# Two-layer encoder trunk: the first two projection units run interleaved, k-tiles of x travel with their weight block, and products with the weights' low parts come last

## The chip, the cores and the metric

One core of a Trainium2 chip runs the whole kernel in one launch. The metric is device time in microseconds (us): the median over several runs. Engines are named as in the profile: PE (TensorE, matmul), PEld (its weight load), DVE (VectorE), ACT (ScalarE), POOL (GpSimd) and SP (SyncE, which here only issues DMAs).

## The reference, cut to what matters

A sequence of 256 frames with 2048 features passes layer A, then layer B. Both attend with 32 heads of 128.

```python
# layer A
h = rms_norm(x, a_norm)
q, k, v, g = split(h @ a_w_in, 4)                 # 2048 -> 4 x 4096
o = chunked_relbias_attention(q, k, v, a_rel_bias)
x = x + (o * silu(g)) @ a_w_out                   # 4096 -> 2048
# layer B
k, v = split(rms_norm(x, kv_norm) @ kv_w, 2)
logf = log_sigmoid(rms_norm(x, kv_norm) @ f_w + f_b)
q, g = split(rms_norm(x, b_norm) @ b_w_in, 2)
o = forgetting_attention(q, k, v, cumsum(logf))
x = x + (o * silu(g)) @ b_w_out
return rms_norm(x, final_norm)
```

Everything is float32. The per-row factor of the RMS norm (`rstd`) is applied after the product `h @ w`, so the projections can begin on `x` times the gain before the norm's sum is known.

## The kernel before, in words

**Products.** A float32 number is split into a high part (rounded to the matmul format `float32r`) and a low part (the rest). A product of two float32 tiles is made of three matmuls: high x high, high x low, low x high. `mm3` (L162-166) issues them for one k-tile (128 rows of the contraction) and one half `t` of the 256 frames. The stationary operand is a 128x128 tile of `x` (`xTh`, `xTl`); the moving one is a k-tile of weights of 512 columns.

**Units and blocks.** A unit is one 512-column slab of a projection: 16 k-tiles in layer A's and B's input projections. A unit has two PSUM accumulators, `acc[0]` and `acc[1]`, one for each half of the frames; the pool holds four. Weights come in blocks of two k-tiles (512 KB, `KB = 2`), so an input unit has 8 blocks of 12 matmuls. Layer A runs 32 units in the order `aqk0, avg0, aqk1, avg1, ...`: `aqk` gives q and k of two heads, `avg` gives v and gate of the same two. `Unit.step(b)` (L259) takes the next block from the feed and issues its 12 matmuls: for each k-tile, first half `t = 0` (three matmuls), then half `t = 1`.

**The feed.** `Feed` walks a list of (unit, block), `todo`, in the order in which the blocks are used. `load` (L178) allocates one of three raw buffers (`RAW = 3`) and issues the DMA on SP. `prepare` (L190) splits a block: ACT copies raw to `hi` (L204), DVE subtracts to get `lo` (L205); there are four slots each of `hi` and `lo` (`SPLIT = 4`), and preparation runs up to four blocks ahead. So the DMA of block n+3 waits for DVE's `lo` of block n, and the split of block n+4 waits for PE to finish block n.

**The start.** `x`, transposed, comes by `load_xT` (L427), and `split_xT` splits it (high part on ACT L142, or on DVE L140 for the first two k-tiles; low part on DVE L143). In the kernel before, k-tiles 0 to 3 are split between the first weight blocks, 4 to 7 after, and 8 to 15 come in two loads of four k-tiles each; the generator `first()` splits them and issues the loads of `x` in row layout (`xs`, 1 MB for each half, L449), from which `norm_a` (L434) makes the sums of squares on DVE and then `rstd` (L102 to L114, with a square root on ACT).

**The attention chain of a pair of heads.** It runs beside the units, in steps of a generator (`side_a`, `attention`):

1. ACT evacuates the `aqk` accumulators times `rstd` into `qk` (L317).
2. `turn` (L308, L312) transposes: DVE turns 32x32 pieces into `Y`, and POOL issues 16 DMAs that carry them into `Z`. Both have one buffer.
3. ACT and DVE split the turned q and k (`wideh`, `widel`, `q1h`, `q1l`: L326, L327), and PE makes the scores `s1p`, `s0p` (L331 to L333, L353).
4. DVE adds the bias and takes the maximum; ACT makes the exponentials (L363); ACT scales the gate (L374); a second `turn` (`sgY`, `sgZ`) transposes both.
5. ACT and DVE split the turned probabilities (`wideh`, `widel` again), PE multiplies them with v (`op`, L331 to L333, L386), and DVE multiplies with the gate (`oT`, L390), which frees `Z` for the next pair of heads.

`QK_STEPS` and `PV_STEPS` say after which block of the unit that PE is working on each of these steps is handed out. The place of each instruction in its engine's queue is then decided by a scheduler when the program is built, not by the text of the code alone. Each engine works through its queue in order.

Of the kernel before, what the change touches and what calls it, by code (L numbers as in the profile page):

```python
# [16 lines left out]
P = 128  # L17
S = 256
NT = S // P
# [11 lines left out]
KD = D // P  # L31
# [4 lines left out]
UN = 512  # L36
KB = 2
# [3 lines left out]
SPLIT = 4  # L41
DEPTH = 3
LATE = 8
KEPT = 5
BIG = 8
TERMS = 8
# [3 lines left out]
QK_STEPS = {0: 1, 6: 1, 7: 2}  # L50
PV_STEPS = {0: 1, 6: 1, 7: 2}
# [4 lines left out]
def r32(ap):  # L56
    return ap.bitcast(F32)
# [3 lines left out]
def trunk(ctx, tc, x, x_t, gains, a_w_in, a_rel, a_w_out, kv_w, f_w, f_b, b_w_in, b_w_out, final_norm, out):  # L61
    nc = tc.nc
    pe, act, dve, pool, sp = nc.tensor, nc.scalar, nc.vector, nc.gpsimd, nc.sync
# [16 lines left out]
    xf = x.rearrange("b (t p) d -> p (b t) d", p=P)  # L80
# [19 lines left out]
    def rstd_of(ssq, name):  # L100
        v = small.tile([P, NT], F32, name=f"v_{name}", tag="rs_v")
        dve.tensor_scalar(v, ssq, 1.0 / D, EPS, op0=OP.mult, op1=OP.add)  # L102
        sd = small.tile([P, NT], F32, name=f"sd_{name}", tag="rs_sd")
        act.activation(sd, v, AF.Sqrt)
# [9 lines left out]
        dve.tensor_scalar(hr, r, 0.5, None, op0=OP.mult)  # L114
        return r, hr
# [17 lines left out]
    def finish(side):  # L133
        advance(side, 99)
# [22 lines left out]
                split_x(dst, banks[c // 2][:, c % 2 * S:(c % 2 + 1) * S], k0 + c, g0)  # L157
            yield

    done = []  # L160

    def mm3(acc, lhs, k, t, hi, lo, nk):  # L162
        ts = slice(t * P, (t + 1) * P)
        pe.matmul(acc[t], lhs.h(k)[:, ts], hi, start=k == 0, stop=False)  # L164
        pe.matmul(acc[t], lhs.h(k)[:, ts], lo, start=False, stop=False)  # L165
        done.append(pe.matmul(acc[t], lhs.l(k)[:, ts], hi, start=False, stop=k == nk - 1))  # L166

    class Feed:

# [2 lines left out]
        def __init__(self, todo):  # L172
            self.todo = iter(todo)
            self.ready, self.loaded = [], []
            self.splits = []

        def load(self, spec, b, first):
            raw = stream.tile([P, KB, UN], F32, name=f"{spec['name']}_raw{b}", tag="raw", bufs=RAW)  # L178
            for j in range(KB) if first else [slice(None)]:
                if first:  # L180
                    first(j)
                sp.dma_start(out=raw[:, j], in_=spec["w"][b][:, j])
            return raw

        def begin(self, first=None):
            spec, b = next(self.todo, (None, 0))
            if spec:
                self.loaded.append((spec, b, self.load(spec, b, first)))

        def prepare(self, ahead=True, parts=(slice(None),)):  # L190
            if not self.loaded:
                self.begin()
            if not self.loaded:
                return
            spec, b, raw = self.loaded.pop(0)
            nm, h = spec["name"], b - (spec["nk"] // KB - spec["late"])
            if 0 <= h < spec["kept"]:
                both = big_tile([P, 2, KB, UN], F32R, f"{nm}_keep{b}")
                hi, lo = both[:, 0], both[:, 1]
            else:  # L200
                hi = stream.tile([P, KB, UN], F32R, name=f"{nm}_hi{b}", tag="hi", bufs=SPLIT)
                lo = stream.tile([P, KB, UN], F32R, name=f"{nm}_lo{b}", tag="lo", bufs=SPLIT)
            for j in parts:
                act.activation(hi[:, j], raw[:, j], AF.Copy)  # L204
                self.splits.append(dve.tensor_sub(lo[:, j], raw[:, j], r32(hi[:, j])))  # L205
# [25 lines left out]
    qkvg, todo = [], []  # L231
    for g in range(NG):
        qkvg.append(spec(f"aqk{g}", a_w_in[2 * g], KD))
        qkvg.append(spec(f"avg{g}", a_w_in[2 * g + 1], KD))
    ao = [spec(f"ao{u}", a_w_out[u], KI) for u in range(4)]
    for sp_ in qkvg + ao:
# [11 lines left out]
    feed = Feed(todo)  # L248
    order = iter(qkvg)

    class Unit:
# [8 lines left out]
        def step(self, b):  # L260
            hi, lo = feed.get()
            hold = b >= self.nk // KB - self.late
            if hold:
                self.held.append((b, hi, lo))
            for j in range(KB):
                for t in range(1 if hold else NT):
                    mm3(self.acc, self.lhs, b * KB + j, t, hi[:, j], lo[:, j], self.nk)
            self.left -= 1
            if not self.left:
                for b, hi, lo in self.held:  # L270
                    for j in range(KB):
                        mm3(self.acc, self.lhs, b * KB + j, 1, hi[:, j], lo[:, j], self.nk)

    def unit(lhs):
        u = Unit(lhs, next(order))
        for b in range(u.nk // KB):
            u.step(b)
            yield u.acc

# [153 lines left out]
    def norm_a():  # L433
        junk = att.tile([P, UN], F32, name="junk", tag="tb")  # L434
        for q in range(4):
            cs = slice(q * UN, (q + 1) * UN)
            for t in range(NT):
                dve.scalar_tensor_tensor(junk, xs[t][:, cs], 1.0, xs[t][:, cs],
                                         op0=OP.mult, op1=OP.mult, accum_out=ssq[:, t, q:q + 1])
        tot = const.tile([P, NT], F32, name="tot")  # L440
        dve.tensor_reduce(tot, ssq, axis=AX.X, op=OP.add)
        return rstd_of(tot, "a")

    def first():

        for k in range(4, KD, 2):
            split_xT(k, k + 2)
            if k < 8:
                sp.dma_start(out=xs[k // 2 - 2], in_=xf[:, k // 2 - 2])  # L449
            if k == KD - 2:  # L450
                rs.extend(norm_a())
            yield

    def halves():
        yield 0
        split_xT(1, 2, True)
        yield 1

    load_xT(0, 1)
    feed.begin(lambda j: load_xT(1, 2) if j else None)  # L460
    load_xT(2, 4)
    feed.begin()
    split_xT(0, 1, True)
    feed.prepare(False, halves())
    load_xT(4, 6)
    feed.begin()
    split_xT(2, 4)
    feed.prepare(False)
    load_xT(6, 8)
# [6 lines left out]
    rs = []  # L476
    ahead = first()

    oA = Stat("oA", KI)

# [32 lines left out]
    prev = None  # L513
    for g in range(NG):
        accs = {}
        accs["qk"] = drive(unit(xT),
                           prev if g else ahead, PV_STEPS if g else {i: 1 for i in range(7)})
        if g == 0:
            finish(ahead)
            rsA, halfA = rs  # L520
        finish(prev)
# [145 lines left out]
    prev = None  # L667
    fg = forget()
    for g in range(NG):
        accs = {}  # L670
# [4 lines left out]
        prev = side_b(g, accs)  # L675
# [96 lines left out]
```

## Time and profile before

| | us |
|---|---|
| median of 3 runs (lowest, highest) | 1859.43 (1858.83, 1859.74) |
| the profiled execution's own time | 1860.0 |
| its span, first to last instruction | 1858.3 |
| PE busy | 1840.2 |
| DVE busy | 1123.8 |
| ACT busy | 1008.2 |
| POOL busy | 542.6 |

The mean granted TensorE clock of the profiled execution is 0.996 of full speed, and the core's DMA engines move 214 GB/s on average, 281 GB/s in the first fortieth of the span. How to read a timeline row: start in us from the span's start, duration, engine, source line, operation, output <- inputs, size, how many instructions were merged into the row, and in brackets how long the engine had been idle and what ended that idle time. A matmul's duration overlaps the next one's, so the distance between starts is what counts.

### The profile page before, as it was taken

To read this page: it belongs to the slowest core of one execution; us is meant where nothing else is said; L and a number is where in the kernel's file an instruction comes from. 1 tells how busy PE (TensorE), PEld (TensorE's weight loads), DVE (VectorE), ACT (ScalarE), POOL (GpSimd) and SP (SyncE) were. 2 spreads that over 40 slices of the span, in tenths; PEclk is the share of its full clock that TensorE was granted. 3 is DMA by queue.
4 is the path that set the end of the run, shared out by engine and by line. 5 is a ranking of instruction groups with operands and counts; after the bars stand their busy time and mean duration, and the time that the engine had idled before them with its cause. 6 is when DMAs were issued, how large, how long until landed. Compare 5 with 4: busy or idle time off the path is not lost.

```text
span 1858.3 us, 25119 instructions
## 1 busy us (share of the span) xinstructions
PE 1840.2 (99%) x8395; PEld 1525.3 (82%) x8395; DVE 1123.8 (60%) x1450; ACT 1008.2 (54%) x1688; POOL 542.6 (29%) x1129
## 2 busy tenths in 40 slices
PE   8999999999999999999999999999999999999998
PEld 6888888888888888887888888888888888888886
DVE  6666656666666666555665666666665665655554
ACT  5555555555555555545555555555555655554443
POOL 0433333333333333111103333333333333333000
PEclk9999999999999999999999999999999999999999
DMA  8666666666676666666767666666666666676664
GB/s 281 216 216 210 212 214 219 214 208 217 215 212 210 217 215 212 208 218 222 230 185 220 209 216 215 216 217 213 214 214 218 214 213 213 212 235 214 207 203 161
DMA packets 141970, 398.43 MB, mean 214 GB/s; under 512 B 31088, under 2 KB 35472, under 8 KB 141456
## 3 DMA queue, kind: packets, MB, share of 16 engines
q1 hardware_dynamic: 106816, 356.35, 60.3%
q0 software_dynamic: 34304, 39.39, 6.6%
q8 instruction: 67, 1.10, 0.2%
q10 hardware_dynamic: 720, 1.07, 0.2%
q14 instruction: 63, 0.52, 0.1%
HBM read 353.15 MB, written 4.23 MB: 192 GB/s over the span
## 4 chain that ended last, share of the span: by engine, by line
PE 88%; DMA 5%; DVE 2%; POOL 2%; ACT 2%; issue 1%; SPq 0%; ACTq 0%; POOLq 0%; DVEq 0%
PE avg_acc L164 6%; PE bqg_acc L164 6%; PE bqg_acc L166 6%; PE bqg_acc L165 6%; PE avg_acc L165 6%; PE avg_acc L166 6%; PE bkv_acc L164 5%; PE bkv_acc L165 5%; PE bkv_acc L166 5%; PE aqk_acc L166 5%; PE aqk_acc L164 5%; PE aqk_acc L165 5%; PE bo_acc L166 3%; PE bo_acc L165 3%; PE bo_acc L164 3%; DMA sgZ<-sgY 2%
## 5 line engine op out<-in xcount | busy, mean ns | idle before, releaser
L312 POOL DMA_DIRECT2D sgZ<-sgY x512 | 250.5, 497 | 467.9 <-DVE sgY L308 410.1
L312 POOL DMA_DIRECT2D qkZ<-qkY x512 | 251.0, 497 | 379.4 <-DVE vl L405 97.3
L205 DVE TENSOR_TENSOR avg_lo<-avg_raw,avg_hi 128x1024 fp32r<-128x1024 f32 x128 | 156.5, 1223 | 130.3 <-ACT avg_hi L204 130.2
L205 DVE TENSOR_TENSOR bqg_lo<-bqg_raw,bqg_hi 128x1024 fp32r<-128x1024 f32 x128 | 156.6, 1223 | 129.4 <-ACT bqg_hi L204 129.4
L204 ACT ACTIVATE bqg_hi<-bqg_raw 128x1024 fp32r<-128x1024 f32 x128 | 135.4, 1058 | 143.2 <-PE bqg_acc L166 85.1
L204 ACT ACTIVATE avg_hi<-avg_raw 128x1024 fp32r<-128x1024 f32 x128 | 135.3, 1057 | 141.3 <-PE avg_acc L166 84.0
L205 DVE TENSOR_TENSOR aqk_lo<-aqk_raw,aqk_hi 128x1024 fp32r<-128x1024 f32 (+1 forms) x129 | 155.3, 1211 | 88.3 <-ACT aqk_hi L204 88.2
L164 PE MATMUL aqk_acc<-aqk_hi,xTh 128*128 128x512 f32 x512 | 202.2, 396 | 3.3 <-ACT xTh L142 3.0
L205 DVE TENSOR_TENSOR bkv_lo<-bkv_raw,bkv_hi 128x1024 fp32r<-128x1024 f32 x128 | 155.3, 1219 | 77.0 <-ACT bkv_hi L204 76.7
L166 PE MATMUL aqk_acc<-aqk_hi,xTl 128*128 128x512 f32 x512 | 200.6, 392 | 1.1 <-DVE xTl L143 1.1
L165 PE MATMUL aqk_acc<-aqk_lo,xTh 128*128 128x512 f32 x512 | 200.6, 392 | 1.1 <-DVE aqk_lo L205 1.1
L164 PE MATMUL bkv_acc<-bkv_hi,xkvh 128*128 128x512 f32 x512 | 201.1, 393 | 0.0
L164 PE MATMUL avg_acc<-avg_hi,xTh 128*128 128x512 f32 x512 | 200.7, 392 | 0.0
L164 PE MATMUL bqg_acc<-bqg_hi,xbh 128*128 128x512 f32 x512 | 200.7, 392 | 0.0
L166 PE MATMUL bqg_acc<-bqg_hi,xbl 128*128 128x512 f32 x512 | 199.5, 390 | 0.0
L166 PE MATMUL bkv_acc<-bkv_hi,xkvl 128*128 128x512 f32 x512 | 199.5, 390 | 0.0
L166 PE MATMUL avg_acc<-avg_hi,xTl 128*128 128x512 f32 x512 | 199.4, 389 | 0.0
L165 PE MATMUL bqg_acc<-bqg_lo,xbh 128*128 128x512 f32 x512 | 199.3, 389 | 0.0
L165 PE MATMUL avg_acc<-avg_lo,xTh 128*128 128x512 f32 x512 | 199.3, 389 | 0.0
L165 PE MATMUL bkv_acc<-bkv_lo,xkvh 128*128 128x512 f32 x512 | 199.2, 389 | 0.0
L204 ACT ACTIVATE aqk_hi<-aqk_raw 128x1024 fp32r<-128x1024 f32 (+1 forms) x129 | 134.8, 1050 | 86.2 <-PE aqk_acc L166 46.0
L204 ACT ACTIVATE bkv_hi<-bkv_raw 128x1024 fp32r<-128x1024 f32 x128 | 134.6, 1057 | 72.8 <-PE bqg_acc L166 41.9
(193 smaller groups left out, 3451.8 us busy)
## 6 DMA issues: line engine op xcount, KB each, us to landing
avg_raw<-in_a_w_in SPq DMA_DIRECT2D x128, 512.0 KB, 4.2
bqg_raw<-in_b_w_in SPq DMA_DIRECT2D x128, 512.0 KB, 4.2
bkv_raw<-in_kv_w SPq DMA_DIRECT2D x128, 512.0 KB, 4.2
aqk_raw<-in_a_w_in SPq DMA_DIRECT2D x127, 512.0 KB, 4.1
ao_raw<-in_a_w_out SPq DMA_DIRECT2D x64, 512.0 KB, 4.3
bo_raw<-in_b_w_out SPq DMA_DIRECT2D x64, 512.0 KB, 4.1
sgZ<-sgY POOLq DMA_DIRECT2D x512, 40.0 KB, 3.9
qkZ<-qkY POOLq DMA_DIRECT2D x512, 32.0 KB, 3.6
```

Of the source, the lines that this page charges most:

```text
L164: pe.matmul(acc[t], lhs.h(k)[:, ts], hi, start=k == 0, stop=False)
L165: pe.matmul(acc[t], lhs.h(k)[:, ts], lo, start=False, stop=False)
L166: done.append(pe.matmul(acc[t], lhs.l(k)[:, ts], hi, start=False, stop=k == nk - 1))
L204: act.activation(hi[:, j], raw[:, j], AF.Copy)
L205: self.splits.append(dve.tensor_sub(lo[:, j], raw[:, j], r32(hi[:, j])))
L312: pool.dma_start(out=z[j * SQ:(j + 1) * SQ, i], in_=y[i * SQ:(i + 1) * SQ, j])
```

## The change

Four edits go together.

- **Order of blocks.** The first two units, `aqk0` and `avg0`, hold all four accumulators at once. Their first blocks alternate (`WOVEN`): `aqk0` block 0, `avg0` 0, `aqk0` 1, `avg0` 1, then `aqk0` 2 to 7, and then the remaining six of `avg0`.
- **x with its block.** Each pair of x's k-tiles is loaded right ahead of the `aqk0` block that needs it, and is split right ahead of that block's split (`feed.also`). No load takes four k-tiles any more.
- **Row layout and norm.** The two loads of `xs` are issued after steps 3 and 5 of the woven list (`XS_STEPS`), and the norm's sums go half by half after the later steps.
- **Order of the three products.** `mm3` takes both halves `t` and issues high x high for both, then low x high for both, and the products with the weights' low part last. This holds for the whole kernel.

The steps of the first pair's attention chain are handed out over the six remaining blocks of `avg0` instead of eight.

```diff
+XS_STEPS = (3, 5)
+WOVEN = [(0, 0), (1, 0), (0, 1), (1, 1)] + [(0, b) for b in range(2, 8)]
...
-    def mm3(acc, lhs, k, t, hi, lo, nk):
-        ts = slice(t * P, (t + 1) * P)
-        pe.matmul(acc[t], lhs.h(k)[:, ts], hi, start=k == 0, stop=False)
-        pe.matmul(acc[t], lhs.h(k)[:, ts], lo, start=False, stop=False)
-        done.append(pe.matmul(acc[t], lhs.l(k)[:, ts], hi, start=False, stop=k == nk - 1))
+    def mm3(acc, lhs, k, ts, hi, lo, nk):
+
+        for i, (x, w) in enumerate(((lhs.h(k), hi), (lhs.l(k), hi), (lhs.h(k), lo))):
+            for t in ts:
+                pe.matmul(acc[t], x[:, t * P:(t + 1) * P], w,
+                          start=k == 0 and i == 0, stop=k == nk - 1 and i == 2)
...
-                self.loaded.append((spec, b, self.load(spec, b, first)))
+                load, split = self.also.get((spec["name"], b), (None, None))
+                if load:
+                    load()
+                self.loaded.append((spec, b, self.load(spec, b, first), split))
...
-            spec, b, raw = self.loaded.pop(0)
+            spec, b, raw, also = self.loaded.pop(0)
+            if also:
+                also()
...
+    woven = [(qkvg[u], b) for u, b in WOVEN]
+    todo = woven + [i for i in whole(qkvg[1]) if i not in woven]
...
-        for q in range(4):
-            cs = slice(q * UN, (q + 1) * UN)
-            for t in range(NT):
+        for t in range(NT):
+            for q in range(4):
+                cs = slice(q * UN, (q + 1) * UN)
                 dve.scalar_tensor_tensor(junk, xs[t][:, cs], 1.0, xs[t][:, cs],
                                          op0=OP.mult, op1=OP.mult, accum_out=ssq[:, t, q:q + 1])
+            yield
...
-    def first():
-
-        for k in range(4, KD, 2):
-            split_xT(k, k + 2)
-            if k < 8:
-                sp.dma_start(out=xs[k // 2 - 2], in_=xf[:, k // 2 - 2])
-            if k == KD - 2:
-                rs.extend(norm_a())
-            yield
...
+    for i in range(1, KD // KB):
+        feed.also[qkvg[0]["name"], i] = (lambda k=i * KB: load_xT(k, k + KB),
+                                         lambda k=i * KB: split_xT(k, k + KB))
     load_xT(0, 1)
     feed.begin(lambda j: load_xT(1, 2) if j else None)
-    load_xT(2, 4)
     feed.begin()
-    split_xT(0, 1, True)
-    feed.prepare(False, halves())
-    load_xT(4, 6)
     feed.begin()
-    split_xT(2, 4)
-    feed.prepare(False)
-    load_xT(6, 8)
-    feed.begin()
-    feed.prepare(False)
-    load_xT(8, 12)
-    feed.begin()
-    load_xT(12, 16)
-    feed.prepare()
+    feed.prepare(parts=halves())
...
+    def woven_units():
+
+        us = [Unit(xT, next(order)) for _ in range(2)]
+        norm = norm_a()
+        for i, (u, b) in enumerate(WOVEN):
+            us[u].step(b)
+            if i in XS_STEPS:
+                sp.dma_start(out=xs[XS_STEPS.index(i)], in_=xf[:, XS_STEPS.index(i)])
+            elif i > XS_STEPS[-1]:
+                next(norm, None)
+        finish(norm)
+        return us
...
-        accs["vg"] = drive(unit(xT), prev, QK_STEPS)
+        accs["vg"] = drive(vg, prev, QK_STEPS if g else {0: 1, 4: 1, 5: 2})
```

What the scheduler makes of it, at three places. First ACT's queue in the first unit, from the sixth block of `aqk0` on in the kernel before (`hi` is a weight block's high part, `xTh` the high part of a k-tile of x, the number names the buffer):

```order
L204 ACTIVATE aqk_hi_181<-aqk_raw_143 128x1024
L204 ACTIVATE aqk_hi_204<-aqk_raw_150 128x1024
L204 ACTIVATE aqk_hi_226<-aqk_raw_152 128x1024
L142 ACTIVATE xTh_98<-xr_102,gain 128x256 x5
L204 ACTIVATE aqk_hi_248<-aqk_raw_185 128x1024
L142 ACTIVATE xTh_98<-xr_102,gain 128x256 x3
```

and in the changed kernel, from the block that needs k-tiles 4 and 5:

```order
L144 ACTIVATE xTh_97<-xr_101,gain 128x256 x2
L211 ACTIVATE aqk_hi_181<-aqk_raw_145 128x1024
L144 ACTIVATE xTh_97<-xr_101,gain 128x256 x2
L211 ACTIVATE aqk_hi_204<-aqk_raw_156 128x1024
L144 ACTIVATE xTh_98<-xr_102,gain 128x256 x2
L211 ACTIVATE aqk_hi_227<-aqk_raw_163 128x1024
```

Before, the splits of three weight blocks stood ahead of the split of k-tile 8, which the first of those blocks needs; now each pair of k-tiles stands directly ahead of its block.

Second PE's queue where the first pair's `op` stands, in the kernel before at the seam between `aqk1` and `avg1`:

```order
L165 MATMUL aqk_acc_572<-aqk_lo_672,xTh_98 128x512
L166 MATMUL aqk_acc_572<-aqk_hi_671,xTl_100 128x512
L331 MATMUL op<-wideh,vh 128x256
L332 MATMUL op<-widel,vh 128x256
L333 MATMUL op<-wideh,vl 128x256
L386 MATMUL op<-sgZ,v_562 128x128
```

and in the changed kernel, in the second block of `avg1`:

```order
L166 MATMUL avg_acc_771<-avg_lo_710,xTh_97 128x512
L342 MATMUL op<-wideh,vh 128x256
L166 MATMUL avg_acc_772<-avg_lo_710,xTh_97 128x512
L166 MATMUL avg_acc_771<-avg_hi_709,xTh_97 128x512
L343 MATMUL op<-widel,vh 128x256
L344 MATMUL op<-wideh,vl 128x256
L397 MATMUL op<-sgZ,v_564 128x128
```

Counted from the start of the queue, 288 of the units' matmuls stand ahead of the first `op` before, and 305 in the changed kernel. In the same way the scores `s1p` have moved from behind 192 of them to behind 219; from the second pair of heads on, both stand where they stood.

Third DVE's queue around the first pair's second turn, before:

```order
L308 STREAM_TRANSPOSE sgY<-sg 128x1280
L205 TENSOR_TENSOR aqk_lo_636<-aqk_raw_525,aqk_hi_635 128x1024
L205 TENSOR_TENSOR aqk_lo_654<-aqk_raw_577,aqk_hi_653 128x1024
L205 TENSOR_TENSOR aqk_lo_672<-aqk_raw_621,aqk_hi_671 128x1024
L205 TENSOR_TENSOR avg_lo_690<-avg_raw_639,avg_hi_689 128x1024
L205 TENSOR_TENSOR avg_lo_708<-avg_raw_657,avg_hi_707 128x1024
L327 TENSOR_TENSOR widel<-sgZ,wideh 128x256 x2
L205 TENSOR_TENSOR avg_lo_732<-avg_raw_675,avg_hi_731 128x1024
L308 STREAM_TRANSPOSE qkY<-qk 128x1024
L390 TENSOR_TENSOR oT<-op,sgZ 128x256 x2
```

and in the changed kernel, from three blocks behind that turn on:

```order
L212 TENSOR_TENSOR avg_lo_734<-avg_raw_677,avg_hi_733 128x1024
L212 TENSOR_TENSOR avg_lo_774<-avg_raw_695,avg_hi_773 128x1024
L319 STREAM_TRANSPOSE qkY<-qk 128x1024
L338 TENSOR_TENSOR widel<-sgZ,wideh 128x256 x2
L212 TENSOR_TENSOR avg_lo_812<-avg_raw_713,avg_hi_811 128x1024
L401 TENSOR_TENSOR oT<-op,sgZ 128x256 x2
```

The transpose of the next pair's q and k now stands ahead of the `widel` that the first pair's `op` takes; it writes the one buffer `Y`, which the 16 DMAs of the second turn read.

More of the change, by code (lines that the diff above doesn't have):

```diff
@@ L175, in __init__ @@
             self.splits = []
+            self.also = {}
         def load(self, spec, b, first):
@@ L229, in whole @@
         return [(spec, b) for b in range(spec["nk"] // KB)]
-    qkvg, todo = [], []
+    qkvg = []
     for g in range(NG):
@@ L234, in trunk @@
         qkvg.append(spec(f"avg{g}", a_w_in[2 * g + 1], KD))
+    woven = [(qkvg[u], b) for u, b in WOVEN]
+    todo = woven + [i for i in whole(qkvg[1]) if i not in woven]
     ao = [spec(f"ao{u}", a_w_out[u], KI) for u in range(4)]
-    for sp_ in qkvg + ao:
+    for sp_ in qkvg[2:] + ao:
         todo += whole(sp_)
@@ L265, in step @@
             for j in range(KB):
-                for t in range(1 if hold else NT):
-                    mm3(self.acc, self.lhs, b * KB + j, t, hi[:, j], lo[:, j], self.nk)
+                mm3(self.acc, self.lhs, b * KB + j, range(1 if hold else NT), hi[:, j], lo[:, j], self.nk)
             self.left -= 1
@@ L271, in step, with rest @@
                     for j in range(KB):
-                        mm3(self.acc, self.lhs, b * KB + j, 1, hi[:, j], lo[:, j], self.nk)
+                        mm3(self.acc, self.lhs, b * KB + j, [1], hi[:, j], lo[:, j], self.nk)
     def unit(lhs):
-        u = Unit(lhs, next(order))
-        for b in range(u.nk // KB):
+        yield from rest(Unit(lhs, next(order)))
+    def rest(u):
+        for b in range(u.nk // KB - u.left, u.nk // KB):
             u.step(b)
@@ L434, in norm_a @@
         junk = att.tile([P, UN], F32, name="junk", tag="tb")
-        for q in range(4):
-            cs = slice(q * UN, (q + 1) * UN)
-            for t in range(NT):
+        for t in range(NT):
+            for q in range(4):
+                cs = slice(q * UN, (q + 1) * UN)
                 dve.scalar_tensor_tensor(junk, xs[t][:, cs], 1.0, xs[t][:, cs],
                                          op0=OP.mult, op1=OP.mult, accum_out=ssq[:, t, q:q + 1])
+            yield
         tot = const.tile([P, NT], F32, name="tot")
         dve.tensor_reduce(tot, ssq, axis=AX.X, op=OP.add)
-        return rstd_of(tot, "a")
-    def first():
-        for k in range(4, KD, 2):
-            split_xT(k, k + 2)
-            if k < 8:
-                sp.dma_start(out=xs[k // 2 - 2], in_=xf[:, k // 2 - 2])
-            if k == KD - 2:
-                rs.extend(norm_a())
-            yield
-    def halves():
-        yield 0
-        split_xT(1, 2, True)
-        yield 1
+        rs.extend(rstd_of(tot, "a"))
+        yield
+    def halves():
+        for j in range(KB):
+            split_xT(j, j + 1, True)
+            yield j
+    for i in range(1, KD // KB):
+        feed.also[qkvg[0]["name"], i] = (lambda k=i * KB: load_xT(k, k + KB),
+                                         lambda k=i * KB: split_xT(k, k + KB))
     load_xT(0, 1)
     feed.begin(lambda j: load_xT(1, 2) if j else None)
-    load_xT(2, 4)
     feed.begin()
-    split_xT(0, 1, True)
-    feed.prepare(False, halves())
-    load_xT(4, 6)
     feed.begin()
-    split_xT(2, 4)
-    feed.prepare(False)
-    load_xT(6, 8)
-    feed.begin()
-    feed.prepare(False)
-    load_xT(8, 12)
-    feed.begin()
-    load_xT(12, 16)
-    feed.prepare()
-    rs = []
-    ahead = first()
+    feed.prepare(parts=halves())
     oA = Stat("oA", KI)
@@ L511, in drive @@
         return acc
-    prev = None
+    def woven_units():
[9 more added lines that the diff above has]
+        return us
+    rs, prev = [], None
     for g in range(NG):
         accs = {}
[L516 to L519, printed above, removed]
+        if g:
+            accs["qk"], vg = drive(unit(xT), prev, PV_STEPS), unit(xT)
+        else:
+            first, second = woven_units()
             rsA, halfA = rs
+            accs["qk"], vg = first.acc, rest(second)
         finish(prev)
```

1 line of the change is left out of this document (removed).

## Prediction

> **What bounds the kernel now.** I read the page first. PE is busy for all but 18 us of the span, so only what takes time from PE in a place, or gives it back there, can move the end.
>
> ```profile
> span 1858.3 us, 25119 instructions
> PE 1840.2 (99%) x8395; PEld 1525.3 (82%) x8395; DVE 1123.8 (60%) x1450; ACT 1008.2 (54%) x1688; POOL 542.6 (29%) x1129
> ```
>
> Next the view of waits, PE alone, whole span: who was waited for, us in total, times, longest.
>
> ```profile
> PE aqk_acc L164 <- ACT xTh L142: 3.0, 1, 3.0
> PE aqk_acc L166 <- DVE xTl L143: 1.1, 1, 1.1
> PE ao_acc L165 <- DVE ao_lo L205: 0.8, 1, 0.8
> ```
>
> The largest waits are in `aqk`, the first unit. The PE timeline gives the place and the price: first matmul of unit 0, the end of its longest wait, the first four of unit 1, and the scores behind unit 1.
>
> ```profile
> 4.86 0.96 PE L164 MATMUL aqk_acc<-aqk_hi,xTh 128*128 128x512 f32 x2
> ...
> 22.02 0.58 PE L164 MATMUL aqk_acc<-aqk_hi,xTh 128*128 128x512 f32 x1 [2.99 <-ACT xTh L142]
> ...
> 37.01 0.39 PE L164 MATMUL avg_acc<-avg_hi,xTh 128*128 128x512 f32 x1
> 37.23 0.39 PE L165 MATMUL avg_acc<-avg_lo,xTh 128*128 128x512 f32 x1
> 37.46 0.39 PE L166 MATMUL avg_acc<-avg_hi,xTl 128*128 128x512 f32 x1
> 37.69 0.39 PE L164 MATMUL avg_acc<-avg_hi,xTh 128*128 128x512 f32 x1
> ...
> 58.77 0.28 PE L331 MATMUL s1p<-wideh,q1h 128*128 128x256 f32 x1
> ```
>
> Unit 1 takes (58.77 - 37.01)/96 = 0.2267 us per matmul without a gap: the pitch. Two units are 192 x 0.2267 = 43.5 us, but they took 58.77 - 4.86 = 53.9. So 10.4 us are lost, all in unit 0. A third of that isn't waiting. The table by stretches of 2 us (PE, PEld, DVE, ACT, POOL busy, granted clock, DMA share, GB/s) has the clock at half behind the 3 us hole:
>
> ```profile
> 22.00:24.00 2.00, 1.00 (x2) 0.30 (x2) 1.90 (x5) 1.57 (x4) 0.00 (x0) 0.58 1.06 393
> 24.00:26.00 2.00, 1.92 (x5) 1.55 (x6) 2.00 (x6) 1.76 (x4) 0.00 (x0) 0.50 0.98 403
> 26.00:28.00 2.00, 2.00 (x6) 1.63 (x5) 2.00 (x5) 0.49 (x2) 0.00 (x0) 0.50 1.02 408
> 28.00:30.00 2.00, 2.00 (x8) 1.55 (x7) 1.93 (x6) 1.06 (x1) 0.00 (x0) 0.72 0.83 290
> ```
>
> The clock is low from about 22.2 to 29.1, near 6.8 us, and half of that, some 3.3 us, is lost work.
>
> **The woven start.** ACT's timeline shows the splits of weight blocks and x:
>
> ```profile
> 6.59 0.63 ACT L204 ACTIVATE aqk_hi<-aqk_raw 128x512 fp32r<-128x512 f32 x1 [1.79 <-DMA aqk_raw<-in_a_w_in]
> 8.62 1.06 ACT L204 ACTIVATE aqk_hi<-aqk_raw 128x1024 fp32r<-128x1024 f32 x1 [0.40 <-DMA aqk_raw<-in_a_w_in]
> 21.48 2.09 ACT L142 ACTIVATE xTh<-xr,gain 128x256 fp32r<-128x256 f32 x5
> 24.24 1.06 ACT L204 ACTIVATE aqk_hi<-aqk_raw 128x1024 fp32r<-128x1024 f32 x1 [0.66 <-DMA aqk_raw<-in_a_w_in]
> ```
>
> The hole at 19 to 22 goes: k-tile 8 no longer stands behind three weight blocks on ACT (first piece of order), and a woven start asks for four weight blocks with two pairs of k-tiles, so x is needed half as fast. What stays: block 0's second half still reaches PE at 6.59 + 0.63, so six of its matmuls start at about 7.28 and not at 4.86 + 6 x 0.2267 = 6.22: 1.06 us. `avg0`'s first block is ready between 8.3 (ACT free at 7.2, plus 1.06) and 9.7 (where the second block was); PE comes at 8.64: 0 to 1.0, I take 0.3, since its load is queued before 256 KB of x that went first until now. Its `lo` comes 1.2 later and four matmuls cover 0.9: 0.3. Later blocks: from 8.62 to 24.24 seven blocks were split 2.6 us apart, with DMA near full; PE takes 12 x 0.2267 = 2.72 for one, so 0 to 1.0 remains over all, I take 0.2. Sum 1.9 (1.1 to 3.4): the two units end at 4.86 + 43.5 + 1.9 = 50.3 instead of 58.77, **8.5 us sooner** (7.0 to 9.3).
>
> **What is late next.** The first pair's attention chain starts from the norm and doesn't speed up with PE. Its rows before, DVE and ACT:
>
> ```profile
> 36.91 0.17 DVE L102 TENSOR_SCALAR v_a<-tot 128x2 f32<-128x2 f32 x1
> 37.21 1.06 ACT L204 ACTIVATE avg_hi<-avg_raw 128x1024 fp32r<-128x1024 f32 x1 [1.66 <-PE aqk_acc L166]
> 38.28 1.28 ACT L104 ACT_TABLE_LOAD   x1
> 40.81 0.17 DVE L114 TENSOR_SCALAR half_a<-rstd_a 128x2 f32<-128x2 f32 x1
> 55.63 0.42 ACT L326 ACTIVATE wideh<-qkZ 128x256 fp32r<-128x256 f32 x1 [3.76 <-DMA qkZ<-qkY]
> 57.21 0.49 ACT L326 ACTIVATE q1h<-qkZ 128x128 fp32r<-128x128 f32 x2
> 66.68 1.51 DVE L308 STREAM_TRANSPOSE sgY<-sg 128x1280 f32<-128x1280 f32 x1
> 81.07 0.72 ACT L326 ACTIVATE wideh<-sgZ 128x256 fp32r<-128x256 f32 x2 [3.45 <-DMA sgZ<-sgY]
> 81.80 0.28 PE L331 MATMUL op<-wideh,vh 128*128 128x256 f32 x1
> 83.25 0.48 PE L164 MATMUL avg_acc<-avg_hi,xTh 128*128 128x512 f32 x1
> ```
>
> Before, PE met `s1p` at 58.77, 1.3 us behind `q1h`'s first half, and `op` the moment `wideh` was there: the chain had no slack even then.
>
> *The norm comes later.* On SP the second half of x in row layout now follows twelve weight blocks, not eight, and SP waits in order: each of those loads waits for DVE's `lo` of three blocks earlier. The ninth block's `lo` is done near 8.64 + 1.2 + 7 x 2.3 to 2.6 = 26 to 28. x then takes
>
> ```profile
> x<-in_x SPq DMA_DIRECT2D x2, 1024.0 KB, 7.0
> ...
> 27.85 0.68 DVE L438 SCALAR_TENSOR_TENSOR junk<-x 128x512 f32<-128x512 f32 x1
> ```
>
> 7.0 us, so 33 to 35; four sums of 0.73, one `lo` (1.2) and 0.4 end in `v_a` at 37.6 to 39.6, against 36.91. From there to `half_a` it was 3.9 us, of which 2.3 are a weight block and a table load on ACT that need not wait for `v_a` now; one more `lo` stands in between: 2.8 to 4. So `half_a` is at 40.4 to 43.6; I take 42.0, 1.2 later than before.
>
> *Scores.* The rest to `wideh` is unchanged, 14.8 us: 56.8. No weight block stands inside the split now: `q1h` at +1.0, 57.8. PE gets there at 50.3 + 27 x 0.2267 = 56.4 and waits 1.4.
>
> *Second turn.* From `s1p` to the end of the `sgY` transpose it was 66.68 + 1.51 - 58.77 = 9.4; nine unit matmuls stand among the scores now and hold ACT's next slot back, so 9.4 to 10.2, I take 10. From there to `wideh` the turn took 12.9 here; later pairs:
>
> ```profile
> 111.78 1.51 DVE L308 STREAM_TRANSPOSE sgY<-sg 128x1280 f32<-128x1280 f32 x1
> 125.64 0.73 ACT L326 ACTIVATE wideh<-sgZ 128x256 fp32r<-128x256 f32 x2 [1.73 <-DMA sgZ<-sgY]
> ...
> 157.71 1.51 DVE L308 STREAM_TRANSPOSE sgY<-sg 128x1280 f32<-128x1280 f32 x1
> 173.64 0.73 ACT L326 ACTIVATE wideh<-sgZ 128x256 fp32r<-128x256 f32 x2 [3.79 <-DMA sgZ<-sgY]
> ```
>
> 12.3 and 14.4. With 12.9 and 0.4 for the first half of `wideh`, `op` can start at 57.8 + 10 + 12.9 + 0.4 = 81.1. PE meets it 86 unit matmuls and about 1 us of scores behind `s1p`, at 57.8 + 20.5 = 78.3, and waits 2.8. Then DVE (third piece): the next pair's transpose, 1.25 us, is ahead of `widel`, and two unit matmuls cover 0.45 of it: 0.7 more.
>
> *What is left.* `op`'s group ends near 81.1 + 0.45 + 0.7 + 1.3 = 83.5; it ended at 83.25. But 307 unit matmuls are then done, not 288: 19 x 0.2267 = 4.3, less 0.25: **4.0 us of the 8.5 remain**. Each us by which the chain is earlier or later adds or takes one, up to the 8.5. The bounds above give 1.5 to 7. The next pair's scores had slack (`wideh` 0.72 and half of `q1h` behind 99.30, that is 100.2, against 105.13):
>
> ```profile
> 99.30 0.72 ACT L326 ACTIVATE wideh<-qkZ 128x256 fp32r<-128x256 f32 x2 [3.79 <-DMA qkZ<-qkY]
> ...
> 105.13 0.28 PE L331 MATMUL s1p<-wideh,q1h 128*128 128x256 f32 x1
> ```
>
> so a chain less than 1 us sooner and a PE 4 us sooner still meet without a further loss.
>
> **Low parts last.** The pitch stays, as matmuls with the same stationary operand (37.01 to 37.23) and with another one (37.23 to 37.46) stood equally far apart, and the page counts as many weight loads (PEld) as matmuls. A wait for a late `lo` falls 0.68 us later (three more matmuls ahead): the 0.8 at `ao_lo` shrinks by up to 0.7. Against that, in layer A ACT now runs one of the two instructions that make the gate
>
> ```profile
> 60.99 0.84 ACT L416 ACTIVATE gs<-avg_acc,half_a 128x256 f32<-128x256 f32 x2
> ```
>
> (0.42) between the exponentials and the gate scaling: up to 0.4 for each pair whose `op` comes late already. I count -0.7 and +1.2, bounds -1 and +3.
>
> Sum: 1860.0 - 4.0 + 0.5 = 1856.5 for the profiled execution, 3.5 less. The median shown lies 0.6 below that execution: 1859.43 - 3.5 = **1855.9**.
>
> **Rivals.**
>
> 1. *Chain in time.* If x lands early and both turns are quick, PE keeps 6.5 to 8.5: 1851 to 1853. For it: table load and block may be done before `v_a`. Against: all early bounds together give only 3. Chance 0.13.
> 2. *The clock halves once more.* The wait at `op` is 2.8 plus 0.7 with 0.45 of work between; a hole of 3 us cost 3.3 us of clock above. Then 0.2 us remain: 1859.2. It decides when a hole of about 3 us falls as the one at 19 did. [...] Chance 0.20.
> 3. *The feed doesn't keep up*, so the waits only move into the woven steps and the norm is later too: gain 0 to 1, 1858.9. For it: DMA is at 0.98 to 1.06 of its share from 22 to 28. Chance 0.08.
> 4. *Slower: alternating banks.* `mm3` now changes its PSUM accumulator at each matmul, not each third. If that leaves gaps, 7680 unit matmuls pay: 1 ns is 7.7 us, so from 0.5 ns on it eats the gain; 1.5 ns gives 1855.9 + 11.5 = 1867.4. Against it: at the change of accumulator (37.46 to 37.69) the distance is the same 0.23. [...] Chance 0.07.
>
> The forecast has the remaining 0.52.
>
> **Numbers.** About 0.2% (3.7 us) is what can be told from no change, so faster means below 1855.7. The forecast's own spread (1853.5 to 1858) lies on both sides, slightly more above: 0.52 x 0.48 = 0.25, plus rival 1's 0.13 and a little of rival 2: 0.41. Slower than 1863.1 is rival 4: 0.07. Within: 0.52. Range 1851.8 to 1859.8: it takes in rivals 2 and 3 and half of 1.
>
> **What would show it.** Right: no wait of PE on `xTh`; clock 1.00 between 20 and 30; `avg0` done near 50; then waits of PE for ACT of about 1.4 at `s1p` and 2.8 at `op`, which starts near 81; `half_a` near 42. Wrong: `op` before 79 or without a wait (rival 1), a clock below 1 at 80 to 90 (rival 2), waits on `hi` between 12 and 45 (rival 3), a pitch above 0.2267 (rival 4).

## The result, and the profile after

The changed kernel takes 1903.18 us (median of 5 runs, 1901.81 to 1904.91) against 1859.43 (5 runs, 1857.07 to 1859.93): ratio 1.0236, 95% interval 1.0224 to 1.0247. It is 44 us slower; 3.5 us faster was forecast. The profiled execution took 1904.91 us.

The page of the changed kernel, span and engines; then the share of the engines in the chain of work that ended last:

```profile
span 1903.2 us, 25143 instructions
PE 1860.1 (98%) x8395; PEld 1532.4 (81%) x8395; DVE 1130.2 (59%) x1450; ACT 1001.1 (53%) x1688; POOL 550.5 (29%) x1129
...
PE 69%; DMA 10%; POOL 6%; DVE 4%; ACT 4%; issue 2%; POOLq 0%; ACTq 0%; DVEq 0%
```

PE is idle for 43 us of the span, before for 18, and a quarter of the last chain now runs over DMA, POOL, DVE and ACT, the engines of the attention chain. The view of waits of PE names the place:

```profile
PE op L342 <- ACT wideh L337: 24.8, 19, 2.7
PE s1p L342 <- ACT q1h L337: 4.4, 1, 4.4
...
PE aqk_acc L166 <- ACT aqk_hi L211: 0.4, 1, 0.4
```

The waits on `xTh` are gone. In their place PE waits 24.8 us, nineteen times, for the split of the second turn; before that was 0.6 us. Where the time came in shows in the first `s1p` of a pair. PE's timeline, first before, for layer B's first pair and its last; then after, for the first two pairs and the same two:

```profile
1003.30 0.28 PE L331 MATMUL s1p<-wideh,q1h 128*128 128x256 f32 x1
...
1694.60 0.28 PE L331 MATMUL s1p<-wideh,q1h 128*128 128x256 f32 x1
```

```profile
61.37 0.58 PE L342 MATMUL s1p<-wideh,q1h 128*128 128x256 f32 x1 [4.43 <-ACT q1h L337]
...
105.95 0.28 PE L342 MATMUL s1p<-wideh,q1h 128*128 128x256 f32 x1
...
1029.84 0.28 PE L342 MATMUL s1p<-wideh,q1h 128*128 128x256 f32 x1
...
1739.12 0.28 PE L342 MATMUL s1p<-wideh,q1h 128*128 128x256 f32 x1
```

Against before, the second pair (105.13 then) is 0.8 us later, layer B's first pair 26.5, the last pair 44.5. So the loss isn't in the start: it grows by about 1.7 us with every pair of layer A and by 1.2 with every pair of layer B.

What a pair now does differently is seen on ACT. First before, the second pair, whose first `s1p` starts at 105.13; then after, the same pair, with `s1p` at 105.95:

```profile
105.70 0.83 ACT L416 ACTIVATE gs<-avg_acc,half_a 128x256 f32<-128x256 f32 x2
106.41 1.07 ACT L204 ACTIVATE aqk_hi<-aqk_raw 128x1024 fp32r<-128x1024 f32 x1
107.76 0.51 ACT L363 ACTIVATE sg<-sg,nm 128x256 f32<-128x256 f32 x1 [0.28 <-DVE nm L361]
...
109.53 1.04 ACT L204 ACTIVATE aqk_hi<-aqk_raw 128x1024 fp32r<-128x1024 f32 x1
110.48 1.26 ACT L374 ACTIVATE sg<-gs,csc 128x128 f32<-128x128 f32 x4
```

```profile
105.70 1.06 ACT L211 ACTIVATE aqk_hi<-aqk_raw 128x1024 fp32r<-128x1024 f32 x1 [0.50 <-PE avg_acc L166]
...
107.38 0.48 ACT L427 ACTIVATE gs<-avg_acc,half_a 128x256 f32<-128x256 f32 x1
109.62 1.06 ACT L211 ACTIVATE aqk_hi<-aqk_raw 128x1024 fp32r<-128x1024 f32 x1 [1.77 <-PE aqk_acc L166]
110.59 0.49 ACT L374 ACTIVATE sg<-sg,nm 128x256 f32<-128x256 f32 x1
...
113.65 1.26 ACT L385 ACTIVATE sg<-gs,csc 128x128 f32<-128x128 f32 x4
```

Before, the weight block ahead of the exponentials (106.41) takes the slot that `avg` left, and starts without a wait. The next block, which needs the slot of `aqk`'s own first block, runs at 109.53, behind the exponentials. After, that next block stands ahead of them: ACT reaches it at 107.86, waits 1.77 us until PE has used `hi` of `aqk`'s first block for the last time, and the exponentials start at 110.59, 4.64 us behind `s1p` instead of 2.63. DVE shows the same a step earlier. Before, the bias (L360) ran as soon as the scores were there, and the next `lo` behind it:

```profile
106.11 0.69 DVE L360 SCALAR_TENSOR_TENSOR sg<-s1p,tb 128x512 f32<-128x512 f32 x1 [0.47 <-PE s1p L333]
...
108.63 1.22 DVE L205 TENSOR_TENSOR aqk_lo<-aqk_raw,aqk_hi 128x1024 fp32r<-128x1024 f32 x1
```

After, the `lo` of the block before that one (106.79) stands ahead of the bias (L371) and the maximum. The last row is the `sgY` transpose, which starts the second turn:

```profile
106.79 1.23 DVE L212 TENSOR_TENSOR aqk_lo<-aqk_raw,aqk_hi 128x1024 fp32r<-128x1024 f32 x1 [0.34 <-ACT aqk_hi L211]
107.93 0.68 DVE L371 SCALAR_TENSOR_TENSOR sg<-s1p,tb 128x512 f32<-128x512 f32 x1
...
114.95 1.51 DVE L319 STREAM_TRANSPOSE sgY<-sg 128x1280 f32<-128x1280 f32 x1
```

It ends 10.5 us behind `s1p` (114.95 + 1.51 - 105.95); before it was 8.2 (111.78 + 1.51 - 105.13). If nothing holds it up, PE comes to `op` 22.97 us behind `s1p`, as before, and the turn takes about as long as before (12.3 us for this pair then, 12.7 now). So in this pair 2.0 us of room have become a wait:

```profile
129.62 0.38 PE L342 MATMUL op<-wideh,vh 128*128 128x256 f32 x1 [0.55 <-ACT wideh L337]
```

### The profile page after: what moved, and what is told of

It reads as the page before. It is cut to its first block, busy times and chain, and to the rows that moved or that the text cites. A ratio compares the mean times of both kernels' runs of the same rounds, so it can differ in the third digit from the quotient of the medians.

```text
span 1903.2 us, 25143 instructions
## 1 busy us (share of the span) xinstructions
PE 1860.1 (98%) x8395; PEld 1532.4 (81%) x8395; DVE 1130.2 (59%) x1450; ACT 1001.1 (53%) x1688; POOL 550.5 (29%) x1129
## 4 chain that ended last, share of the span: by engine, by line
PE 69%; DMA 10%; POOL 6%; DVE 4%; ACT 4%; issue 2%; POOLq 0%; ACTq 0%; DVEq 0%
PE bqg_acc L166 18%; PE avg_acc L166 17%; DMA sgZ<-sgY 10%; PE bo_acc L166 9%; PE ao_acc L166 8%; PE bkv_acc L166 7%; POOL sgZ L323 6%; PE aqk_acc L166 4%; DVE sgY L319 2%; ACT sg L374 2%; PE op L397 1%; DVE aqk_lo L212 1%; PE op L343 1%; PE s0p L364 1%; DVE bkv_lo L212 1%
## 5 line engine op out<-in xcount | busy, mean ns | idle before, releaser
L166 PE MATMUL aqk_acc<-aqk_hi,xTh 128*128 128x512 f32 x512 | 159.9, 393 | 0.4 <-ACT aqk_hi L211 0.4
L166 PE MATMUL bqg_acc<-bqg_hi,xbh 128*128 128x512 f32 x512 | 159.5, 393 | 0.0
L166 PE MATMUL bkv_acc<-bkv_hi,xkvh 128*128 128x512 f32 x512 | 159.4, 392 | 0.0
L166 PE MATMUL avg_acc<-avg_hi,xTl 128*128 128x512 f32 x512 | 159.1, 392 | 0.0
L166 PE MATMUL aqk_acc<-aqk_lo,xTh 128*128 128x512 f32 x512 | 158.4, 390 | 0.1
L166 PE MATMUL aqk_acc<-aqk_hi,xTl 128*128 128x512 f32 x512 | 158.5, 390 | 0.0
L166 PE MATMUL bqg_acc<-bqg_lo,xbh 128*128 128x512 f32 x512 | 158.5, 390 | 0.0
L166 PE MATMUL bqg_acc<-bqg_hi,xbl 128*128 128x512 f32 x512 | 158.5, 390 | 0.0
L166 PE MATMUL bkv_acc<-bkv_hi,xkvl 128*128 128x512 f32 x512 | 158.0, 390 | 0.0
L166 PE MATMUL bkv_acc<-bkv_lo,xkvh 128*128 128x512 f32 x512 | 157.9, 389 | 0.0
```

The lines of the kernel that those rows point to most:

```text
L166: pe.matmul(acc[t], x[:, t * P:(t + 1) * P], w, start=k == 0 and i == 0, stop=k == nk - 1 and i == 2)
```

## The experiments

Two theories were set against each other. **A**: the new order of the three products costs the time, by way of the queues of ACT and DVE. **B**: the woven start makes the first pair late, and the later pairs inherit that. Two more were watched: **C**, that the change of accumulator at every matmul costs it, and, later, **D**, that the order on PE itself or the later release of `lo` does, whatever stands in the queues.

**One half of the change at a time.** `start_only` is the changed kernel with

```diff
-        for i, (x, w) in enumerate(((lhs.h(k), hi), (lhs.l(k), hi), (lhs.h(k), lo))):
-            for t in ts:
-                pe.matmul(acc[t], x[:, t * P:(t + 1) * P], w,
-                          start=k == 0 and i == 0, stop=k == nk - 1 and i == 2)
+        for t in ts:
+            s = slice(t * P, (t + 1) * P)
+            pe.matmul(acc[t], lhs.h(k)[:, s], hi, start=k == 0, stop=False)
+            pe.matmul(acc[t], lhs.h(k)[:, s], lo, start=False, stop=False)
+            pe.matmul(acc[t], lhs.l(k)[:, s], hi, start=False, stop=k == nk - 1)
```

> The changed kernel with the three products in the order of the kernel before (for each half: high x high, high x low weight, low x high); the woven start, x with its block and the later norm stay. Theory A (the loss comes from the product order, which puts one more weight block ahead of the exponentials on ACT and makes each pair's chain 2.0 to 2.4 us longer): exponentials start 2.6 us after s1p in later pairs, the sgY transpose ends at s1p + 8.2, no repeated clock falls, time 1853 to 1860. Rival B (the woven start makes the first pair late and all later pairs inherit it): waits at op in nearly every pair as in the changed kernel, 1895 to 1905.

Measured: 1858.56 us (11 runs), ratio 0.9996 (0.9987 to 1.0005): no difference from before. Exponentials start at `s1p` + 2.63 again, and the last pair's scores stand at 1694.8.

`order_only` is the kernel before with the new `mm3` and nothing else:

```diff
-                for t in range(1 if hold else NT):
-                    mm3(self.acc, self.lhs, b * KB + j, t, hi[:, j], lo[:, j], self.nk)
+                mm3(self.acc, self.lhs, b * KB + j, range(1 if hold else NT), hi[:, j], lo[:, j], self.nk)
```

> The kernel before with only the new order of the three products (both halves together, low weights last); its start is that of before. Theory A: exponentials start 4.6 us after s1p, the sgY transpose ends at s1p + 10.2 to 10.5, PE waits at op for about 20 us in all, the clock falls several times, time 1895 to 1908. Rival B (the start): 1857 to 1862, waits at op as before (2 us in all).

Measured: 1900.91 us (5 runs), ratio 1.0217 (1.0195 to 1.0239). The profiled execution was the slowest of the five (1908.52). Waits of PE and ACT's timeline of its third pair (`s1p` at 154.01):

```profile
PE op L329 <- ACT wideh L324: 23.9, 17, 3.4
```

```profile
155.44 0.47 ACT L414 ACTIVATE gs<-avg_acc,half_a 128x256 f32<-128x256 f32 x1
157.69 1.06 ACT L203 ACTIVATE aqk_hi<-aqk_raw 128x1024 fp32r<-128x1024 f32 x1 [1.78 <-PE aqk_acc L164]
158.66 0.49 ACT L361 ACTIVATE sg<-sg,nm 128x256 f32<-128x256 f32 x1
```

The same block with the same wait stands ahead of the exponentials, 4.65 us behind `s1p`, with the old start. B falls; the product order alone carries the loss (40 us here, 44 in the changed kernel).

**Which part of the product order.** `pair_low_mid` keeps the halves paired and only puts the low weights in the middle; `half_low_last` keeps them last and finishes each half by itself:

```diff
-        for i, (x, w) in enumerate(((lhs.h(k), hi), (lhs.l(k), hi), (lhs.h(k), lo))):
+        for i, (x, w) in enumerate(((lhs.h(k), hi), (lhs.h(k), lo), (lhs.l(k), hi))):
```

```diff
-        for i, (x, w) in enumerate(((lhs.h(k), hi), (lhs.l(k), hi), (lhs.h(k), lo))):
-            for t in ts:
...
+        for t in ts:
+            s = slice(t * P, (t + 1) * P)
+            pe.matmul(acc[t], lhs.h(k)[:, s], hi, start=k == 0, stop=False)
+            pe.matmul(acc[t], lhs.l(k)[:, s], hi, start=False, stop=False)
+            pe.matmul(acc[t], lhs.h(k)[:, s], lo, start=False, stop=k == nk - 1)
```

> The changed kernel, halves still paired (a new accumulator at every matmul), but the product with the weights' low part in the middle: high x high, high x low weight, low x high. Theory A (low weights last: hi is free for the next block three matmuls sooner, and lo only after the last matmul): exponentials start 2.6 us after s1p as before, time as start_only, 1853 to 1860. Rival C (the alternation of the two accumulators costs it): 1895 to 1905.

> The changed kernel with each half finished by itself, but its product with the weights' low part last (high x high, low x high, high x low for half 0, then the same for half 1): hi is free one matmul sooner than before instead of two. Theory A: part of the loss, since one weight block more stands ahead of v and the gate on ACT but none between these and the exponentials: 1858 to 1880. Rival C (alternating accumulators cost it): as start_only.

Measured: `pair_low_mid` 1860.08 us (12 runs), ratio 0.9996 (0.9988 to 1.0005); `half_low_last` 1868.11 (5 runs), ratio 1.0040 (1.0026 to 1.0055). With the alternation kept, the loss is gone, so C falls. The times go with the last use of a block's `hi` among its twelve matmuls: at the twelfth (before, `start_only`, `pair_low_mid`) nothing is lost, at the eleventh 0.4% (`half_low_last`), at the tenth 2.2% (the changed kernel's order, which is two matmuls sooner; the text on `pair_low_mid` above says three). The last use of `lo` is the twelfth in both of the slower orders, so it doesn't make the difference between them. That a split is put into ACT's queue the sooner, the sooner PE is done with the high part whose slot it takes, is inferred from the queues seen here.

The 0.4% is not a smaller dose of the same loss, though. In `half_low_last`'s profile (1864.59 us, below its median) one more `hi` stands ahead of `v` and the gate, as expected, but the exponentials start 2.63 us behind `s1p` in most pairs, as before. Of the 3.8 us by which its last scores are later than `start_only`'s, 2.7 are there already at the second pair's (106.87 against 104.14). What costs it that in the first pair wasn't tested.

**The queue against the order on PE.** `pinned` keeps PE's new order and only holds two splits back in the queues: the fourth block's `lo` behind the maximum on DVE, the fifth block's `hi` behind the last exponential on ACT.

```diff
+            behind = pins.pop(b, None)
+            with tc.issue_after(behind.ins) if behind else nullcontext():
+                for j in parts:
+                    act.activation(hi[:, j], raw[:, j], AF.Copy)
+                    self.splits.append(dve.tensor_sub(lo[:, j], raw[:, j], r32(hi[:, j])))
...
+            pins[3] = dve.tensor_reduce(nm[:, t], s_, axis=AX.X, op=OP.max, negate=True)
...
+                pins[4] = act.activation(s_[:, i], s_[:, i], AF.Exp, bias=nm[:, t, i:i + 1],
+                                         accum_out=sm[:, t, i:i + 1])
```

> The changed kernel with its new order of products, and two orders of issue forced for each pair: the fourth weight block behind the scores (counted from the unit that follows them) has its lo behind the last nm on DVE, and the fifth has its hi behind the last exponential on ACT. PE's own order is that of the changed kernel. Theory A in its narrow form (the price is the place of these two blocks in the queues of DVE and ACT): exponentials start 2.6 to 3.4 us after s1p instead of 4.6, the sgY transpose ends at s1p + 8.2 to 9.2 instead of 10.2 to 10.5, waits at op under 6 us in all, time 1857 to 1868. Rival D (the later release of lo, or the new order on PE itself, slows the chain whatever stands ahead of it): 1890 to 1905.

Measured: 1871.37 us (5 runs), ratio 1.0055 (1.0043 to 1.0067). Waits of PE, and ACT in the second pair (`s1p` at 105.85):

```profile
PE op L346 <- ACT wideh L341: 7.2, 7, 1.9
PE s1p L346 <- ACT q1h L341: 3.6, 1, 3.6
```

```profile
107.27 0.47 ACT L431 ACTIVATE gs<-avg_acc,half_a 128x256 f32<-128x256 f32 x1
108.48 0.51 ACT L378 ACTIVATE sg<-sg,nm 128x256 f32<-128x256 f32 x1 [0.73 <-DVE nm L376]
...
110.25 0.45 ACT L431 ACTIVATE gs<-avg_acc,half_a 128x256 f32<-128x256 f32 x1
110.61 1.05 ACT L215 ACTIVATE aqk_hi<-aqk_raw 128x1024 fp32r<-128x1024 f32 x1
```

The exponentials start 2.63 us behind `s1p` again and the `sgY` transpose ends at + 8.5 (layer A) and + 8.2 (layer B). 32 of the 44 us come back with these two queue places in each pair, while PE's order is that of the changed kernel but for a few matmuls around the first pair's scores and `op`; so D can at most own the rest. The time missed the expected 1868 by 3 us, and the waits at `op` the expected 6 by 1.2.

The last pair's scores stand 10.6 us later than in `start_only`'s profile. 1.7 of that are there at the second pair's scores (105.85 against 104.14); in the first pair the `s1p` matmuls lasted 415 to 581 ns, as in the changed kernel at a clock of 0.50 (415 to 582), against 278 to 387 in `start_only`. From there on `op` starts 5.3 us later behind `s1p`, summed over the pairs, the groups of `op` matmuls are 4.7 longer, and 1.2 come back at the seam of the two layers. Two things fit this: the gate instruction at 110.25 puts the transpose 0.36 later in each of layer A's pairs, and the second turn took 13.5 us on average, against 12.9 in `start_only`. Why the turn took longer is open.

**The price is the wait at `op`.** `after_late_op` is the changed kernel with `op` one block later in layer A only:

```diff
-PV_STEPS = {0: 1, 6: 1, 7: 2}
+PV_STEPS = {0: 1, 6: 1}
...
-        finish(prev)
-        prev = side_a(g, accs)
+        old, prev = prev, side_a(g, accs)
...
+            if i == 0:
+                finish(old)
```

> The changed kernel with op and what follows it one block (12 matmuls, 2.7 us) later in layer A; layer B as in the changed kernel. If the chain behind s1p is only 2.2 us longer and the wait at op is its price, layer A's loss goes (the first scores of layer B stood 26.5 us later than before, 1029.8 against 1003.3) and layer B's stays: 1874 to 1884. If the chain has no room anywhere, the wait moves from op to the next s1p: 1895 to 1905.

Measured: 1876.30 us (4 runs), ratio 1.0089 (1.0076 to 1.0102). The exponentials are as late as in the changed kernel (+ 4.64), but layer B's first scores stand at 999.8 instead of 1029.8, 3.5 us sooner than before, and layer B loses its part as in the changed kernel. So the 2.3 us by which layer A's chain is longer cost nothing where `op` has the room for them: what they cost is the room that `op` had.

**What the start could give.** `early_x` is `start_only` with this edit; `best` is `early_x` with the late `op` of layer A:

```diff
-XS_STEPS = (3, 5)
+XS_STEPS = (0, 1)
```

> The woven start with the products in the order of before, and the two loads of x in row layout issued after woven steps 0 and 1 instead of 3 and 5. If the late norm is what ate the woven start's gain: half_a ends at 36 to 40 instead of 45.3, no wait at the first s1p, which stands near 57, the first op near 80 to 81 with a wait under 1, time 1850 to 1855. Rival (the 2 MB of x ahead of the weights starve the woven units, PE waits for hi or xTh 2 to 5 us between 10 and 40): 1857 to 1862. Rival (later pairs' waits take it again whatever the start): 1857 to 1860.

> early_x with op one block (2.7 us) later in layer A, so that slow turns in layer A are covered. Of the waits that layer A's pairs had at op before (S to S of 46.5 to 46.7 instead of 45.9 in 5 of 15 pairs, near 3 us in all) most goes: 2 to 3 us under early_x, 1848 to 1853. Rival: op to the next scores gets 2.7 us shorter, and where qkZ lands late s1p waits instead: same as early_x or 1 to 4 us slower.

Measured: `early_x` 1856.77 us (11 runs), ratio 0.9984 (0.9975 to 0.9992); `best` 1855.26 (12 runs), ratio 0.9976 (0.9966 to 0.9986), the only two versions faster than before, both by less than was expected (1850 to 1855 and 1848 to 1853). Their profiled executions took 1860.20 and 1850.73 us. Waits of PE in `early_x`, then in `best`:

```profile
PE op L343 <- ACT wideh L338: 3.7, 4, 1.7
PE aqk_acc L167 <- DVE aqk_lo L213: 2.2, 3, 1.5
...
PE aqk_acc L168 <- DVE xTl L145: 1.1, 1, 1.1
```

```profile
PE aqk_acc L166 <- ACT aqk_hi L212: 2.2, 2, 1.4
PE aqk_acc L167 <- DVE aqk_lo L213: 1.7, 4, 0.5
```

In `early_x` `half_a` ends at 37.3 and the first `s1p` is met without a wait, at 56.0, as expected, but the first rival has its part: the weights and k-tiles of x behind the 2 MB in row layout come late, and PE waits 4.5 us in the woven units (1.7 in `start_only`). The first `op` is still 1.4 us late, so the second pair's scores stand at 104.0, where `start_only` has 104.1. In `best` there is no wait on `wideh` left, the second pair's scores stand at 101.05 (4.1 sooner than before), and pair follows pair at 45.9 us through layer A. The profiled execution was its fastest; by the ratio of all runs the gain is 4.5 us.

## Why the prediction was wrong, step by step

- **Woven start, PE's side: right.** The clock is 1.00 from 22 to 30, no wait on `xTh` is left, and PE came to `s1p` at 61.37 - 4.43 = 56.9, where 56.4 was said.

```profile
22.00:24.00 2.00, 2.00 (x10) 1.69 (x9) 1.71 (x4) 1.57 (x3) 0.00 (x0) 1.00 0.93 315
...
28.00:30.00 2.00, 2.00 (x11) 1.65 (x10) 1.21 (x4) 1.06 (x1) 0.00 (x0) 1.00 0.98 410
```

- **What is late next: right mechanism, mis-sized.** The two waits at `s1p` and `op` are there. `half_a`, put at 42.0 with 43.6 as the worst, came at 44.68: DVE's and ACT's rows after.

```profile
36.44 0.69 DVE L449 SCALAR_TENSOR_TENSOR junk<-x 128x512 f32<-128x512 f32 x1
...
40.59 0.17 DVE L104 TENSOR_SCALAR v_a<-tot 128x2 f32<-128x2 f32 x1
...
44.68 0.17 DVE L116 TENSOR_SCALAR half_a<-rstd_a 128x2 f32<-128x2 f32 x1
```

```profile
40.66 1.28 ACT L106 ACT_TABLE_LOAD   x1
...
60.39 0.72 ACT L337 ACTIVATE wideh<-qkZ 128x256 fp32r<-128x256 f32 x2 [1.19 <-DMA qkZ<-qkY]
```

  The second half of `x` was summed from 36.4, where 33 to 35 was said for its landing, and the table load, counted as out of the way, ran only at 40.66, so that `v_a` to `half_a` took 4.1, with 3.9 before and 2.8 to 4 said. From `half_a` to `wideh` it took 15.7 instead of 14.8. Together (2.7 and 0.9) `s1p` was 3.6 us later than said. `start_only`, which has only this part, shows the sum: `s1p` at 61.21, `op` at 84.40 where 81.1 was said, and the second pair's scores at 104.14 instead of 105.13. Of the 8.5 us 1.0 was left, not 4.0; by time 0.7 (a gain of 2.4 to a loss of 0.9).

- **Low parts last: this step failed.** It said "I count -0.7 and +1.2, bounds -1 and +3"; `order_only` measured +40 (36 to 44). Of what the new order moves the step had priced the gate instruction, and rightly: `pinned` has 0.36 for the "0.4". It hadn't priced the weight block that moved ahead of the exponentials, nor the one ahead of the maximum, and it had not asked how much room `op` has in later pairs. The rows quoted answered that: `sgY` ends at 113.29, `wideh`'s first half at 125.64 + 0.42, PE comes to `op` at 128.09. That is 2.0 us in this pair, and the chain became 2.3 longer. PE's rows of before, the second pair's `op`, on time, and the third pair's, late by 0.1, each with the first unit matmul behind it:

```profile
128.09 0.28 PE L331 MATMUL op<-wideh,vh 128*128 128x256 f32 x1
...
129.17 0.48 PE L164 MATMUL avg_acc<-avg_hi,xTh 128*128 128x512 f32 x1
...
174.11 0.38 PE L331 MATMUL op<-wideh,vh 128*128 128x256 f32 x1
...
175.79 0.48 PE L164 MATMUL avg_acc<-avg_hi,xTh 128*128 128x512 f32 x1
```

- **How 2.3 us a pair become 44.** From the second pair's scores to the last pair's, the profile is 43.7 us longer. Summed over these 30 pairs, `op` starts 25.7 us later behind its `s1p` (22.7 of it are counted as waits: 24.8 less the first pair's 1.5, against 0.6), the groups of `op` matmuls are 15.3 longer, and the way from there to the next scores 2.7.

  2.3 us against 2.0 of room would be a wait of only 0.3, but the room isn't the same in every pair. Before, the second turn took 11.7 to 14.8 us (here and in the rest of this point without the first pair, the last and the one at the end of layer A), and the room went with it from 2.7 us to none. Taking 2.3 us in layer A and 2.1 in layer B from each pair's own room gives about 21 us of waits, an estimate, against the 23.3 measured (24.8 - 1.5). 21 pairs of 29 reach `op` late (more than 23.0 us behind `s1p`), before 5.

  A late `op` also leaves `widel` uncovered: the group takes 1.68 us when it is late (174.11 to 175.79), against 1.08 on time (128.09 to 129.17). And the granted clock fell to 0.50 four times in or behind such waits, for 17 us in all. That costs at most 8.5 us, half of the 17, which lie within the longer groups and the way to the next scores.

- **Rivals.** 1 (chain in time) and 3 (the feed) did not come: of waits on `hi` 0.4 us are left. 2 (the clock) came, but not at 80 to 90, where the clock was 1.00: it fell to 0.50 once in the wait ahead of the first scores and four times in or behind a wait at a later `op`. 4 (alternating banks) named the right edit and sign and the wrong mechanism: the pitch of two matmuls merged to a row,

```profile
103.68 0.62 PE L166 MATMUL avg_acc<-avg_hi,xTl 128*128 128x512 f32 x2
104.14 0.61 PE L166 MATMUL avg_acc<-avg_lo,xTh 128*128 128x512 f32 x2
```

  is 0.46 / 2 = 0.23 as before, and `pair_low_mid` alternates without a loss.

## What to carry to other kernels

An edit on the engine that sets the time can change when a buffer is released, and with that what stands in the other engines' queues: look for the work whose buffer now comes free sooner, and for what it is put ahead of, in every repetition and not only where the edit was aimed. Before an edit to a loop, write down how much room each meeting point has, and for several turns (here 2.0 us at `op` in one pair, but from 2.7 to none over the pairs); a shift repeats with every turn. Time saved at the start stays saved only if every chain behind it comes sooner too.

## What the runs showed of the hardware

In these runs the length of a wait alone does not tell whether the clock falls. In the changed kernel PE's pause of 1.74 us ahead of `op` at 178.05 was followed by a clock of 0.50, and one of the same length ahead of `op` at 274.48 by 1.00; a pause of 2.65 us ahead of `op` at 418.19 had 0.50 in it and behind it, and one of 2.65 us ahead of `op` at 1715.55 had 1.00. In `start_only` the clock was 1.00 from 58 to 68, with PE's pause of 3.11 us ahead of the first scores (61.21) in it. Four stretches of the changed kernel (PE, PEld, DVE, ACT, POOL busy, granted clock, DMA share, GB/s):

```profile
178.00:179.00 1.00, 0.88 (x4) 0.67 (x4) 0.76 (x2) 1.00 (x2) 0.00 (x0) 0.83 0.31 119
179.00:180.00 1.00, 1.00 (x6) 1.00 (x6) 0.72 (x1) 1.00 (x3) 0.00 (x0) 0.50 0.07 29
...
275.00:277.00 2.00, 2.00 (x13) 1.74 (x14) 1.51 (x3) 1.83 (x3) 0.00 (x0) 1.00 0.05 20
...
419.00:421.00 2.00, 2.00 (x10) 2.00 (x10) 1.26 (x2) 1.54 (x3) 0.00 (x0) 0.50 0.00 0
...
1716.00:1718.00 2.00, 1.99 (x12) 1.77 (x13) 1.51 (x3) 2.00 (x5) 0.00 (x0) 1.00 0.04 12
```

The changed kernel's five falls ahead of its end started at 59.2, 178.7, 417.6, 612.2 and 1619.1 us and lasted 3.4 us three times and 6.8 twice. They began in the pause or, at the latest, 1.4 us behind PE's restart (1617.70 to 1619.1). No run here tested what decides which pause is followed by a fall.
